# A hybrid attention block on one core: tokens loaded features first, the first norm's factor moved to the products, and four smaller edits

## The chip, the core and the metric

The kernel runs on one core of a Trainium2 chip. The metric is the device time of one execution in microseconds (us). The core has TensorE (PE, with its weight loads PEld), VectorE (DVE), ScalarE (ACT), GpSimd (POOL), and a queue of SyncE (SP) that issues every transfer of this kernel. Each engine works through its own list of instructions in order; an instruction that waits for another engine or for a transfer holds up all that stand behind it on its engine.

## What is computed

One encoder layer on 1024 tokens of 1024 features, cut to its steps:

```python
h = rmsnorm(x, norm_mix)                        # x * rsqrt(mean(x*x) + eps) * gain
proj = h @ w_in                                 # 3384 columns, split into 11 parts
qa, ka, va, qi, ki, wi, qb, kb, vb, gdown, ogate = split(proj)
o_a = dsa_mixer(qa, ka, va, qi, ki, wi)         # index scores, 256 best keys of each query, softmax
o_b = gla_mixer(qb, kb, vb, log_sigmoid(gdown @ w_gate_up + b_gate) / 16)
o_b = rmsnorm(o_b, gla_norm) * silu(ogate)
x = x + concat(o_a, o_b) @ w_out
h = rmsnorm(x, norm_ffn)
x = x + (silu(h @ w_ffn_gate) * (h @ w_ffn_up)) @ w_ffn_down
return rmsnorm(x, norm_final)
```

## The kernel before

Every large product is made of three TensorE passes (`mm3`): each operand is split into a high part, rounded by ACT, and a low part, the rest, made by DVE or POOL. So weights and tokens alike go through "ACT high, then DVE or POOL low" before TensorE can use them.

The order on each engine is fixed ahead by a planner in the kernel (`Flow`): each piece of work is a thread that asks for slots (`pg` pages of SBUF, `ps` four PSUM banks, `pl` two PSUM pairs, `hp` half pages), waits for events, and gives the engine with an assumed duration. The planner emits the instructions in the order of its own clock; on the chip that order stands, and the semaphores make up for what takes longer.

- Beginning. `load_x` brings eight tiles of 128 tokens. `first_norm` takes each tile's sum of squares (ACT and DVE in turn), POOL makes the factor `rstd`, DVE scales the tile (L489). `hidden` transposes it on TensorE (`tp`, L522, 64 transposes of 128x128), and `split_hidden` makes `hT`, high on ACT (L496), low on DVE (L498). `small_weights` gathers 88 narrow columns of `w_in` (`wms`, `wm`). `W` stages weights (`st`), with high on ACT (L257) and low on POOL (L262).
- Products of `main`: `misc` (index keys, index weights and gate, from `wm`) and `index_queries` (`qi`) for each half of the tokens, then `proj_t` (`pj`: value and gate columns) and `proj_f` (`pf`: qb and kb, qa, ka). The `evac_...` functions empty the banks. Behind `misc` and `qi` the index scores start, and `choose` finds the 256th best score of each query by counting, 32 rounds on DVE and ACT at the lowest rank, so it fills DVE.
- `gla` (`pa`, `pk`, `pv`, `po`) runs in between the products; its `att` (L1121) empties the pair that `pk` wants next.
- `softmax` starts with the last product of `ka`: logits `lg` in one of two pairs, emptied by DVE (L1337), then exponent (ACT), reciprocal (DVE), scaling (POOL), transposes `ptr`, and the value products `av`. `combine` adds the two halves of a value sum (`lo`, `so`).
- `out_tiles`, `second_norm` and `scale_tile` (`hr`) make the operands of the feed-forward part, `split_b` splits them (`hc`, low L1629), and `products` and `down` follow.

Of the kernel before, what the change touches and what calls it, by code (L numbers as in the profile page):

```python
# [9 lines left out]
F32 = mybir.dt.float32  # L10
# [315 lines left out]
def block_kernel(ctx: ExitStack, tc: tile.TileContext, a: dict, out: bass.AP, dbg=None):  # L326
# [78 lines left out]
    xs = {}  # L405

    def load_x(i):
        xs[i] = page([P, D], F32, "x")
        nc.sync.dma_start(xs[i], x[i * P:(i + 1) * P, :])

    load_x(0)
    mats = cst.tile([P, 6, P], F32, name="mats")
    nc.sync.dma_start(mats[:, 0:1, :], a["c_mats"][:, 0:1, :])
    ident, tri, flip, cmask = (mats[:, i, :] for i in range(4))
    cmi = mats[:, 4:6, :].rearrange("p a n -> p (a n)").bitcast(I32)
    load_x(1)
    nrm = cst.tile([P, 2, KT], F32, name="nrm")
    wms = page([P, KT, P], F32, "wms")
    nc.gpsimd.memset(wms, 0.0)
    wv = w_in.rearrange("(k p) n -> p k n", p=P)  # L420
    with nc.allow_non_contiguous_dma("small"):
        nc.sync.dma_start(nrm[:, 0, :], a["norm_mix"].rearrange("l (k p) -> p (l k)", p=P))
        load_x(2)
        load_x(3)
        nc.sync.dma_start(wms[:, :, 32:72], wv[:, :, C_KI:C_KI + 40])
        nc.sync.dma_start(wms[:, :, 0:32], wv[:, :, C_KI:C_KI + 32])
        nc.sync.dma_start(wms[:, :, 96:112], wv[:, :, C_GD:C_GD + 16])
    for i in range(4, 8):
        load_x(i)

    def more_loads():

        todo = [(mats[:, 1:, :], a["c_mats"][:, 1:, :]), (wgu[96:112, :], w_gu),
                   (bgt, row_bc(a["b_gate"], 256)), (gnb, row_bc(a["gla_norm"], 512)), (tab, a["rel_bias"]),
                   (nrm[:, 1, :], a["norm_ffn"].rearrange("l (k p) -> p (l k)", p=P))]
        yield At(26000.0)
# [12 lines left out]
    junk_v = cst.tile([P, S], BF16, name="junk_v")  # L449

# [14 lines left out]

    wiT = cst.tile([P, NT * 8], F32, name="wiT")
    fl = Flow()
    ev = fl.event
    pg = Slots(fl, NPG - NT - 1)
    hp, kb, ps, pl = (Slots(fl, n) for n in (NHP, NKB, 4, 2))  # L470
    fl.free[DMA] = 16500.0
# [5 lines left out]
    hT = {}  # L477

# [3 lines left out]
    def first_norm(i):  # L482
        yield At((4500.0, 6050.0, 8650.0, 10000.0, 14000.0, 15250.0, 16700.0, 18200.0)[i])
        yield (ACT, act(S) + 140) if i % 2 == 0 else (DVE, dve(S))
        ss = sumsq(xs[i], i % 2 == 0)
        yield POOL, 730
        r = rstd_of(ss, 1, D)
        yield DVE, 660
        nc.vector.tensor_scalar(xs[i], xs[i], r, None, op0=ALU.mult)  # L489
        ev("xn", i).set()  # L490

    def split_hidden(hf, d, b, give):
# [3 lines left out]
        nc.scalar.activation(t[:, 0, :], b, AF.Copy, scale=nrm[:, 0, d:d + 1])  # L496
        yield DVE, dve(HB) + 60
        nc.vector.scalar_tensor_tensor(t[:, 1, :], b, nrm[:, 0, d:d + 1], f32(t[:, 0, :]),  # L498
                                       op0=ALU.mult, op1=ALU.subtract)
        if give is not None:  # L500
            give.give()
        hT[d, hf] = t
        ev("hT", d, hf).set()

    def hidden(hf):

        step = KT if hf == 0 else 2
        for d0 in range(0, KT, step):
            bs = []
            if hf == 0:  # L510
                for _ in range(4):
                    yield ps
                    bs.append((bank("tp"), ps))
            while len(bs) < step:
                yield pl
                w = wide("tp")
                bs += [(w[:, :HB], None), (w[:, HB:], pl)]
            for j in range(4):
                yield ev("xn", hf * 4 + j)
                for d in range(d0, d0 + step):  # L520
                    yield PE, pe(P, 2)
                    nc.tensor.transpose(bs[d - d0][0][:, j * P:(j + 1) * P], xs[hf * 4 + j][:, d * P:(d + 1) * P],  # L522
# [1834 lines left out]
```

## Time and profile before

| | |
|---|---|
| three runs, median | 1287.97 us (1284.92 to 1291.63) |
| the profiled execution | 1289.89 us, span of its trace 1288.1 us, so 1.8 us lie around it |
| TensorE busy | 1243.2 us, 97% of the span |
| DVE, ACT, POOL busy | 933.7, 600.6, 394.5 us |
| mean granted TensorE clock | 0.985 of full speed |
| moved by DMA | 232.06 MB, 180 GB/s over the span |

The span is what the trace shows from the first to the last instruction. An engine's busy time is summed over its own instructions, so a busy TensorE may still run at the lower clock. The granted clock has two levels here, 1.2 GHz (shown as 0.50) and 2.4 GHz (1.00).

### The profile page before, as it was taken

Reading aid. Unit: us, or ns where it says so; the run is one execution under the profiler, and the core shown is the slowest. Engines: PE = TensorE matmul, PEld = TensorE weight load, DVE = VectorE, ACT = ScalarE, POOL = GpSimd, SP = SyncE. Lnnn points to the kernel's source line nnn. Section 1 sums busy time; section 2 is a strip of 40 time slices with the busy share of each in tenths; the row PEclk is TensorE's granted clock in tenths of the full one; section 3 lists DMA queues with packets and bytes.
Section 4 is the critical chain, followed back from the end, with each engine's and each line's share of the span. In section 5 each row is a group of like instructions: output and inputs, shape, how many; then the busy total and the mean of one; then the engine's idle time right before and its main releaser. Section 6 shows DMA issues by size and latency. Waiting matters only on the chain. (4 is left out here: it accounts for less than half of the span.)

```text
span 1288.1 us, 17923 instructions
## 1 busy us (share of the span) xinstructions
PE 1243.2 (97%) x6074; PEld 1022.6 (79%) x6074; DVE 933.7 (72%) x1739; ACT 600.6 (47%) x1113; POOL 394.5 (31%) x375
## 2 busy tenths in 40 slices
PE   6999999999999999899989999999999999999997
PEld 5878878767787998778868787878888888888885
DVE  6389988979964998843688887768778653335875
ACT  4467777634524787621344444444444332222333
POOL 5324335523401544310103334334333120000340
PEclk8999999979999999999989999999999999999999
DMA  6653221334563437683015777767665479555664
GB/s 212 191 150 123 74 74 42 131 138 152 178 221 100 114 85 201 190 270 129 34 61 184 273 245 258 254 246 261 229 219 205 133 258 379 180 196 190 225 238 164
DMA packets 124909, 232.06 MB, mean 180 GB/s; under 512 B 14297, under 2 KB 72465, under 8 KB 124817
## 3 DMA queue, kind: packets, MB, share of 16 engines
q1 hardware_dynamic: 124816, 230.91, 54.4%
q8 instruction: 48, 0.79, 0.3%
q14 instruction: 45, 0.36, 0.1%
HBM read 148.02 MB, written 82.85 MB: 179 GB/s over the span
## 5 line engine op out<-in xcount | busy, mean ns | idle before, releaser
L1626 POOL TENSOR_TENSOR w<-raw,w 128x512 fp32r<-128x512 f32 x60 | 85.3, 1424 | 214.2 <-ACT w L1766 182.3
L1766 ACT ACTIVATE w<-raw 128x512 fp32r<-128x512 f32 x132 | 81.4, 626 | 54.3 <-DMA d_wd<-wd 15.0
L760 DVE TENSOR_SCALAR_CACHE_REDUCE junk_v<-acc,thr 128x768 bf16<-128x768 f32 (+3 forms) x128 | 103.7, 810 | 2.0
L262 POOL TENSOR_TENSOR w<-st,w 128x512 fp32r<-128x512 f32 x52 | 73.4, 1422 | 75.5 <-ACT w L257 73.3
L767 ACT ACTIVATE junk_a<-acc,thr 128x1024 bf16<-128x1024 f32 x64 | 73.4, 1146 | 46.2 <-DVE thr L784 37.5
L2102 DVE TENSOR_TENSOR da<-U,da 128x512 fp32r<-128x512 f32 x54 | 43.1, 799 | 53.7 <-ACT da L2100 53.5
L2100 ACT ACTIVATE da<-U 128x512 fp32r<-128x512 f32 x54 | 33.7, 630 | 98.8 <-PE da L2156 33.2
L372 PE MATMUL pj<-w,hT 128*128 128x512 f32 x192 | 79.2, 412 | 0.0
L2031 ACT ACTIVATE wd<-wd 128x512 fp32r<-128x512 f32 x77 | 48.3, 629 | 62.1 <-DMA d_wd<-wd 28.1
L373 PE MATMUL pj<-w,hT 128*128 128x512 f32 x192 | 75.9, 395 | 0.0
L374 PE MATMUL pj<-w,hT 128*128 128x512 f32 x192 | 75.8, 395 | 0.0
L372 PE MATMUL pf<-hT,w 128*128 128x512 f32 x192 | 75.8, 395 | 0.0
L1347 POOL TENSOR_SCALAR pb<-pb,sume 128x384 f32<-128x384 f32 (+3 forms) x64 | 47.7, 751 | 89.9 <-DVE sume L1345 74.1
L374 PE MATMUL pf<-hT,w 128*128 128x512 f32 x192 | 74.8, 389 | 0.0
L373 PE MATMUL pf<-hT,w 128*128 128x512 f32 x192 | 74.8, 389 | 0.0
L1807 PE MATMUL fb<-hc,w 128*128 128x512 f32 x176 | 69.5, 395 | 3.9 <-DVE gt L1842 2.5
L1808 PE MATMUL fb<-hc,w 128*128 128x512 f32 x176 | 69.2, 393 | 3.8 <-DVE hc L1629 3.8
L1808 PE MATMUL fc<-hc,w 128*128 128x512 f32 x176 | 69.5, 395 | 2.4 <-DVE hc L1629 2.4
L1807 PE MATMUL fc<-hc,w 128*128 128x512 f32 x176 | 69.1, 392 | 0.4 <-DVE gt L1861 0.4
L2156 PE MATMUL da<-db,da 128*128 128x512 f32 x176 | 68.7, 390 | 0.7 <-DVE da L2102 0.7
L1626 POOL TENSOR_TENSOR wd<-wd 128x512 fp32r<-128x512 f32 x33 | 49.8, 1511 | 63.7 <-ACT wd L2031 55.9
L2154 PE MATMUL da<-db,da 128*128 128x512 f32 x176 | 68.6, 390 | 0.6 <-ACT da L2100 0.6
(315 smaller groups left out, 3643.7 us busy)
## 6 DMA issues: line engine op xcount, KB each, us to landing
d_wd<-wd SPq DMA_DIRECT2D x77, 512.0 KB, 3.5
db<-d_wd SPq DMA_DIRECT2D x77, 512.0 KB, 4.3
st<-w_in SPq DMA_DIRECT2D x52, 256.0 KB, 2.8
raw<-w_ffn_gate SPq DMA_DIRECT2D x22, 512.0 KB, 5.2
raw<-w_ffn_up SPq DMA_DIRECT2D x22, 512.0 KB, 4.5
wd<-w_ffn_down SPq DMA_DIRECT2D x44, 256.0 KB, 4.8
d_ux<-gt SPq DMA_DIRECT2D x9, 512.0 KB, 2.6
d_uy<-gt SPq DMA_DIRECT2D x9, 512.0 KB, 3.5
```

Of the source, the lines that this page charges most:

```text
L262: (eng or self.nc.gpsimd).tensor_tensor(w[:, 1, :], st, f32(w[:, 0, :]), op=ALU.subtract)
L372: mm(ps, lh, rh, start=first, stop=False)
L373: mm(ps, lh, rl, start=False, stop=False)
L374: mm(ps, ll, rh, start=False, stop=last)
L760: v.tensor_scalar(junk_v[:, :w], acc[ts[i]], col, float(S - TOPK), op0=ALU.is_ge, op1=ALU.subtract, accum_out=cnt[:, i:i + 1])
L767: nc.scalar.activation(junk_a[:, :NA[t]], acc[t], AF.Sign, bias=thf[:, nv:], scale=-1.0, accum_out=cnt[:, nv:])
L1626: nc.gpsimd.tensor_tensor(dst, src, high, op=ALU.subtract)
L1766: nc.scalar.activation(w4[:, 0], src, AF.Copy)
L1807: mm(b, w[:, 0, kk], h[:, 0, :], start=first, stop=False, skip_group_check=True)
L1808: mm(b, w[:, 0, kk], h[:, 1, :], start=False, stop=False, skip_group_check=True)
L2154: mm(bs[t], l[:, 0, tt], r[:, 0, :], start=first, stop=False, skip_group_check=True)
L2156: mm(bs[t], l[:, 1, tt], r[:, 0, :], start=False, stop=last, skip_group_check=True)
```

## The change

1. The host lays out a transposed copy of `x` (`c_xt`), the narrow columns (`c_wm`) and the two gains (`c_norms`). `xT` tiles (128 features by 512 tokens) are loaded and split into `hT` without the norm's factor; the scaling by L489 and the 64 transposes are gone. The tokens `x` are loaded too, later, for the sums of squares alone.
2. The factor goes to the products: `rs` as a per-token scale in ACT where tokens lie on partitions; where they lie along the row, `rows` spreads it over 128 partitions (`R`, by eight products of 128x128) and DVE multiplies by it while it empties the bank (`misc`, `qi`, qa, qb, kb, ka). For qa the low part goes from DVE to POOL; for qb and kb the copy goes from ACT to DVE.
3. `W.load()` issues three weight loads ahead of the planner's start, which takes them as there from time 0.
4. `combine` copies half of the value sum, and DVE reads the other half from PSUM; the bank is given back after DVE's sums.
5. The low parts of the last pair of keys (`c == 3`) wait for the first softmaxes.
6. `scale_tile` gives half of its work for tokens 0 to 511 to ACT.
7. Eleven products of 128x512 on a zeroed `junk_a`, whose result nobody reads, stand first on TensorE.

```diff
-    load_x(0)
...
-    nc.gpsimd.memset(wms, 0.0)
...
-        nc.sync.dma_start(wms[:, :, 32:72], wv[:, :, C_KI:C_KI + 40])
...
+    load_xt(0, 0)
+    nc.sync.dma_start(nrm, a["c_norms"])
+    load_wm(0)
+    for k in range(1, 4):
+        load_xt(k, 0)
+    load_wm(1)
+    for k in range(4, KT):
+        load_xt(k, 0)
+    nc.sync.dma_start(mats[:, 0:1, :], a["c_mats"][:, 0:1, :])
+    W.load()
...
+    nc.vector.memset(junk_a, 0.0)
+    idle = wide("idle")
+    for _ in range(11):
+        mm(idle[:, :HB], junk_a[:, :P], junk_a[:, :HB], start=True, stop=True)
...
-    fl.free[DMA] = 16500.0
+    fl.free[DMA] = 12000.0
...
+    def split_hidden(k, hf):
+        if hf == 0:
+            yield At(4500.0 + 650.0 * (k + (k > 3)))
+        else:
+            yield ev("xt", k)
         yield pg
         yield ACT, act(HB) + 42
         t = page([P, 2, HB], F32R, "hT")
-        nc.scalar.activation(t[:, 0, :], b, AF.Copy, scale=nrm[:, 0, d:d + 1])
+        nc.scalar.activation(t[:, 0, :], xT[k, hf], AF.Copy, scale=nrm[:, 0, k:k + 1])
...
+    def load_tokens():
+        W.limit = 4
+        for k in range(KT):
+            if k % 2 == 0:
+                yield pg
+            yield DMA, 650
+            load_xt(k, 1)
+            ev("xt", k).set(2500)
+        for i in range(NT):
+            yield pg
+            yield DMA, 1300
+            xs[i] = page([P, D], F32, "x")
+            nc.sync.dma_start(xs[i], x[i * P:(i + 1) * P, :])
+            ev("x", i).set(2500)
+        W.limit = 8
...
+    def rows():
+        yield pl
+        w = wide("rows")
+        for hf in range(2):
+            yield hp
+            m = half([P, 4, P], F32, "rcol")
             for j in range(4):
...
+                yield ev("rs", i)
+                yield DVE, 250
+                nc.vector.tensor_scalar(m[:, j, :], ident, 0.0, rs[:, i:i + 1], op0=ALU.mult, op1=ALU.add)
+                yield PE, 350
+                mm(w[:, i * P:(i + 1) * P], m[:, j, :], ident, start=True, stop=True)
+            hp.give()
+            yield ACT, act(HB)
+            o = slice(hf * HB, (hf + 1) * HB)
+            nc.scalar.activation(R[:, o], w[:, o], AF.Copy)
+            ev("R", hf).set()
+        pl.give()
...
     def evac_qa(hf, c, b):
...
+        nc.vector.scalar_tensor_tensor(q, b, -0.125, R[:, hf * HB:(hf + 1) * HB], op0=ALU.mult, op1=ALU.mult)
+        ps.give()
         yield ACT, act(HB)
...
+        nc.scalar.activation(t[:, 0, :], q, AF.Copy)
+        yield POOL, pool2(HB)
+        nc.gpsimd.tensor_tensor(t[:, 1, :], q, f32(t[:, 0, :]), op=ALU.subtract)
...
-        yield ACT, act(HB)
-        nc.scalar.activation(dst[i][:, o], b, AF.Copy, scale=0.125 if c < 2 else 1.0)
+        yield DVE, dve(HB)
+        nc.vector.scalar_tensor_tensor(dst[i][:, o], b, 0.125 if c < 2 else 1.0, R[:, o], op0=ALU.mult, op1=ALU.mult)
...
+        nc.vector.tensor_tensor(kf, b, R[:, o], op=ALU.mult)
+        ps.give()
         yield ACT, 2 * act(HB)
...
+        if c == 3:
+            yield ev("p", 2 * PAIRS[0] + 1, 1)
         yield DVE, 2 * dve(HB)
...
-        nc.scalar.activation(lo, OP.pop((p, c)), AF.Copy)
-        ps.give()
+        b = OP.pop((p, c))
+        nc.scalar.activation(lo[64:128, :], b[64:128, :], AF.Copy)
...
+            nc.vector.tensor_tensor(so[e * 64:(e + 1) * 64, :], b[0:64, e * 256:(e + 1) * 256],
                                     lo[64:128, e * 256:(e + 1) * 256], op=ALU.add)
+        ps.give()
...
         for d in range(0, 4, 2):
+            if t and d:
+                yield ACT, 500
+                for i in (d, d + 1):
+                    nc.scalar.activation(hr[(d0 + d) // 2, t][:, i - d, o], b3[:, i, :], AF.Copy,
+                                         scale=nrm[:, 1, d0 + i:d0 + i + 1])
+                continue
             yield DVE, dvf(256)
```

Three places where the order on an engine moves. ACT at the program's beginning, before (`junk_a` is the sum of squares, `wm` the narrow columns, `w<-st` a staged weight's high part):

```order
L460 ACT_TABLE_LOAD
L460 ACTIVATE junk_a,ss<-x 128x1024 x2
L537 ACTIVATE wm<-wms 128x1024
L460 ACTIVATE junk_a,ss<-x 128x1024
L496 ACTIVATE hT<-tp,nrm 128x512 x8
L460 ACTIVATE junk_a,ss<-x 128x1024
L257 ACTIVATE w<-st 128x512 x3
```

and in the changed kernel:

```order
L257 ACT_TABLE_LOAD
L257 ACTIVATE w<-st 128x512 x3
L497 ACTIVATE hT<-xT,nrm 128x512
L574 ACTIVATE wm<-wms 128x512
L497 ACTIVATE hT<-xT,nrm 128x512 x3
L574 ACTIVATE wm<-wms 128x512
L497 ACTIVATE hT<-xT,nrm 128x512 x4
L257 ACTIVATE w<-st 128x512
L497 ACTIVATE hT<-xT,nrm 128x512 x8
L463 ACTIVATE junk_a,ss<-x 128x1024 x2
```

The three staged weights, which stood behind the first eight token splits, now stand ahead of them; on SP their loads are issued behind the ten loads of `xT` and `wms`.

DVE at the first softmaxes, before (the rows of L1257 are the keys' low parts, L1337 empties the logits, L1375 makes low parts for the value products):

```order
L1257 SCALAR_TENSOR_TENSOR K<-pf,K 64x512 x12
L1337 ISA pb,mn<-lg,acc 128x384
L1337 ISA mn 128x1
L1337 ISA pb,mn<-lg,acc 128x512
L1337 ISA mn 128x1
L1345 RECIPROCAL sume<-sume 128x1
L1337 ISA pb,mn<-lg,acc 128x384
L1337 ISA mn 128x1
L1257 SCALAR_TENSOR_TENSOR K<-pf,K 64x512 x4
L1345 RECIPROCAL sume<-sume 128x1 x2
```

and in the changed kernel ahead of the first logit (L1310 multiplies by the factor, L1323 makes the low parts, L883 ends a mask):

```order
L1323 TENSOR_TENSOR K<-kf,K 64x512 x4
L883 TENSOR_SCALAR acc<-sign 128x1024
L1310 TENSOR_TENSOR kf<-pf,rows 128x512 x2
L1323 TENSOR_TENSOR K<-kf,K 64x512 x4
L1310 TENSOR_TENSOR kf<-pf,rows 128x512 x2
L1403 ISA pb,mn<-lg,acc 128x384
```

and behind the fourth:

```order
L1411 RECIPROCAL sume<-sume 128x1
L1403 ISA pb,mn<-lg,acc 128x384
L1403 ISA mn 128x1
L1411 RECIPROCAL sume<-sume 128x1 x2
L1403 ISA pb,mn<-lg,acc 128x512
L1403 ISA mn 128x1
L1411 RECIPROCAL sume<-sume 128x1 x3
L1323 TENSOR_TENSOR K<-kf,K 64x512 x4
L1441 TENSOR_TENSOR pt<-ptr,pt 128x256
L1441 TENSOR_TENSOR pt<-ptr,pt 128x128
L1441 TENSOR_TENSOR pt<-ptr,pt 128x512 x2
```

The four low parts move from behind three logits to behind six, right ahead of the first `pt`; two new multiplications stand ahead of the first logit.

DVE between the last `xn` and the first `hc` of the feed-forward part, before:

```order
L1576 TENSOR_SCALAR xn<-y,rstd 128x1024
L1755 TENSOR_TENSOR raw<-raw,s_6539 128x4x128
L1605 TENSOR_TENSOR hr<-tp,nrm 128x2x128 x2
L1663 TENSOR_TENSOR hr<-hr 128x2x128
L1605 TENSOR_TENSOR hr<-tp,nrm 128x2x128
L1667 TENSOR_TENSOR hr<-hr 128x2x128
L1671 TENSOR_TENSOR hr<-hr 128x2x128
L1629 TENSOR_TENSOR w<-raw,w 128x512
L1629 TENSOR_TENSOR w<-s_5611,w 128x512
L1897 TENSOR_TENSOR gt<-fa,gt 128x512
L1663 TENSOR_TENSOR hr<-hr 128x2x128
L1629 TENSOR_TENSOR w<-s_6539,w 128x512
```

and in the changed kernel:

```order
L1643 TENSOR_SCALAR xn<-y,rstd 128x1024
L1828 TENSOR_TENSOR raw<-raw,s_6573 128x4x128
L1678 TENSOR_TENSOR hr<-tp,nrm 128x2x128
L1702 TENSOR_TENSOR w<-raw,w 128x512
L1702 TENSOR_TENSOR w<-s_5604,w 128x512
L1970 TENSOR_TENSOR gt<-fa,gt 128x512
L1702 TENSOR_TENSOR w<-s_6573,w 128x512
L1702 TENSOR_TENSOR hc<-hr,hc 128x512 x4
```

Two of three `hr` scalings and the sums (L1663 to L1671) have left this stretch; the sums stand ahead of `xn`.

## Rows read from the trace of the kernel before

**Rows 1.** Busy time by stretches of 20 us: each engine, clock, DMA share, GB/s

```profile
core 0: us, PE busy (x) PEld busy (x) DVE busy (x) ACT busy (x) POOL busy (x), PEclk, DMA share, GB/s
0.00:20.00 20.00, 8.63 (x38) 7.39 (x39) 11.05 (x17) 10.21 (x16) 9.86 (x18) 0.92 0.87 271
...
120.00:140.00 20.00, 20.00 (x89) 16.54 (x89) 19.35 (x42) 13.18 (x20) 5.67 (x5) 1.00 0.33 103
...
380.00:400.00 20.00, 20.00 (x89) 16.55 (x89) 5.51 (x8) 4.74 (x8) 0.00 (x0) 1.00 0.42 115
...
640.00:660.00 20.00, 13.76 (x53) 10.16 (x52) 16.65 (x35) 9.96 (x20) 0.00 (x0) 0.88 0.00 1
```

**Rows 2.** Waits of TensorE over the span: releaser, total us, times, longest

```profile
PE tp L522 <- DVE x L489: 9.3, 3, 8.5
PE fb L1808 <- DVE hc L1629: 3.8, 1, 3.8
PE lg L1324 <- DVE mn L1337: 3.1, 2, 2.9
PE pk L1102 <- DVE att L1121: 2.9, 1, 2.9
...
PE fc L1808 <- DVE hc L1629: 2.4, 1, 2.4
...
PE pv L1141 <- DVE bit L774: 1.2, 1, 1.2
```

**Rows 3.** Timeline of the beginning: start, duration, engine, count, idle before and releaser

```profile
4.52 1.06 ACT L460 ACTIVATE junk_a<-x 128x1024 bf16<-128x1024 f32 x1 [2.52 <-DMA x<-x]
...
8.54 3.68 PE L522 MATMUL tp<-mats,x 128*128 128x128 f32 x16 [8.54 <-DVE x L489]
...
17.61 0.79 PE L372 MATMUL misc<-hT,wm 128*128 128x512 f32 x1 [2.55 <-DVE hT L498]
...
34.97 1.06 PE L522 MATMUL tp<-mats,x 128*128 128x128 f32 x8
...
52.42 0.39 PE L372 MATMUL pj<-w,hT 128*128 128x512 f32 x1
```

**Rows 4.** Timeline and tile `st`: splits of tokens and weights, merged runs

```profile
15.48 4.71 ACT L496 ACTIVATE hT<-tp,nrm 128x512 fp32r<-128x512 f32 x8
16.80 5.36 DVE L498 SCALAR_TENSOR_TENSOR hT<-tp,nrm,hT 128x512 fp32r<-128x512 f32 x8
21.08 1.71 ACT L257 ACTIVATE w<-st 128x512 fp32r<-128x512 f32 x3
L262 POOL TENSOR_TENSOR w<-st,w x14: 1285/1292/1847, 22.1 to 51.9; 128x512 fp32r<-128x512 f32 x14
```

**Rows 5.** One microsecond of the token loads

```profile
14.00:15.00 1.00, 1.00 (x9) 0.82 (x8) 1.00 (x1) 0.57 (x1) 0.00 (x0) 1.00 1.03 414
```

**Rows 6.** Three stretches at the lower clock

```profile
17.00:23.70 6.70, 6.09 (x14) 4.79 (x15) 6.70 (x10) 5.79 (x11) 3.58 (x6) 0.50 0.38 130
262.80:276.20 13.40, 13.40 (x58) 8.74 (x57) 7.51 (x25) 3.48 (x7) 1.23 (x2) 0.50 0.10 35
...
648.50:651.70 3.20, 3.20 (x8) 2.52 (x9) 1.74 (x4) 0.00 (x0) 0.00 (x0) 0.50 0.02 5
```

**Rows 7.** Timeline at the first softmaxes

```profile
405.17 2.79 DVE L1257 SCALAR_TENSOR_TENSOR K<-pf,K 64x512 fp32r<-64x512 f32 x4
...
408.25 0.69 DVE L1337 CUSTOM_DVE_ANT_0 pb<-lg,acc 128x512 f32<-128x512 f32 x1
...
414.15 0.72 PE L1384 MATMUL av<-pt,V 128*128 128x256 f32 x4
```

**Rows 8.** DVE's timeline at the beginning of the feed-forward part

```profile
646.75 0.68 DVE L1629 TENSOR_TENSOR hc<-hr,hc 128x512 fp32r<-128x512 f32 x1
...
652.14 0.69 DVE L1849 TENSOR_TENSOR gt<-fc,gt 128x512 f32<-128x512 f32 x1 [1.90 <-PE fc L1809]
...
658.40 0.68 DVE L1629 TENSOR_TENSOR hc<-hr,hc 128x512 fp32r<-128x512 f32 x1
```

**Rows 9.** DVE sums of two operands: `so` from SBUF, `hr` from PSUM (ns; us)

```profile
L1405 DVE TENSOR_TENSOR so<-lo x32: 420/422/1129, 418.6 to 553.2; 64x256 f32<-64x256 f32 x32
638.13 0.42 DVE L1605 TENSOR_TENSOR hr<-tp,nrm 128x256 f32<-128x256 f32 x1
```

More of the change, by code (lines that the diff above doesn't have):

```diff
@@ L449, in block_kernel @@
     junk_v = cst.tile([P, S], BF16, name="junk_v")
+    rs = cst.tile([P, NT], F32, name="rs")
     def rstd_of(ss, n, width):
@@ L502, in split_hidden @@
[L502 to L517, printed above, removed]
-            for j in range(4):
[L519 to L522, printed above, removed]
-                                        ident)
-            for d in range(d0, d0 + step):
-                fl.spawn(split_hidden(hf, d, *bs[d - d0]), 0.01 * d)
-        pg.give(n=4)
@@ L529, in block_kernel @@
-    wm, kw = [], []
-    def small_weights():
-        yield At(11200.0)
-        for _ in range(2):
-            yield pg
-        yield ACT, act(S)
-        wm.extend(page([P, KT, P], F32R, "wm") for _ in range(2))
-        nc.scalar.activation(wm[0], wms, AF.Copy)
-        yield DVE, dve(S)
-        nc.vector.tensor_tensor(wm[1], wms, f32(wm[0]), op=ALU.subtract)
-        pg.give()
-        ev("wm").set()
+        hT[k, hf] = t
+        if k % 2:
+            pg.give()
+        ev("hT", k, hf).set()
@@ new lines, in load_tokens, with first_norm @@
+    def load_tokens():
+        W.limit = 4
+        for k in range(KT):
+            if k % 2 == 0:
+                yield pg
[9 more added lines that the diff above has]
+        W.limit = 8
+    def first_norm(i):
+        yield ev("x", i)
+        yield (ACT, act(S) + 140) if i % 2 == 0 else (DVE, dve(S))
+        ss = sumsq(xs[i], i % 2 == 0)
+        pg.give()
+        yield POOL, 730
+        r = small([P, 1], F32, "rstd", 4)
+        nc.gpsimd.tensor_scalar(r, ss, 1.0 / D, EPS, op0=ALU.mult, op1=ALU.add)
+        nc.gpsimd.tensor_tensor(rs[:, i:i + 1], r, mhalf[:, 0:1], op=ALU.pow)
+        ev("rs", i).set()
@@ L626, in index_queries @@
         bs = []
-        for _ in range(2):
-            yield ps
-            bs.append(bank("qi"))
+        if hf == 0:
+            for _ in range(2):
+                yield ps
+                bs.append(bank("qi"))
+        else:
+            yield pl
+            w = wide("qi")
+            bs = [w[:, :HB], w[:, HB:]]
         for k in range(KT):
@@ L1247, in evac_ka @@
         yield ev("ka page", c)
+        yield hp
+        yield DVE, dve(HB)
+        kf = half([P, HB], F32, "kf")
+        nc.vector.tensor_tensor(kf, b, R[:, o], op=ALU.mult)
+        ps.give()
         yield ACT, 2 * act(HB)
```

154 lines of the change are left out of this document (91 added, 63 removed).

## The prediction

> **What bounds the kernel now.** I read the stretches of 20 us first, then the waits of TensorE, then the timeline at each place where it waits. TensorE is busy in nearly every stretch [rows 1], so only three things are worth time: work taken from TensorE, its waits, and the stretches at the lower clock that follow a wait. Waits worth naming [rows 2]: 9.3 us for the scaled tokens, nearly all before the first product; 2.9 and 1.2 us where the gated block `gla` begins; 2.9 us at the first softmaxes; 2.4 and 3.8 us at the beginning of the feed-forward part. Behind them the clock stands at 1.2 GHz for 6.7, 13.4 and 3.2 us [rows 6], each costing half its length. DVE is the engine that most of these waits are for, and it is full where the scores are chosen, 19.35 of 20 us, and nearly free before the softmaxes, 5.51 of 20 [rows 1].
>
> **The beginning.** Before, the first product starts at 17.61 us and `pj` at 52.42 [rows 3]. What is new is the order on ACT: three staged weights stand ahead of the first token split, and their loads stand on SP behind eight of `xT` and two of `wms`. So ACT waits for thirteen loads of 256 KB and a small one, 3.4 MB. The first load of 512 KB was used at 4.52 us [rows 3]; the other 2.9 MB at 414 GB/s [rows 5] take 7 us, which is 11.5 us; I take 12, since that microsecond is one of the best. Then the last staged weight (1.71/3 = 0.57 us), `hT` and `wm` on ACT (4.71/8 = 0.59 each) and two low parts on DVE (5.36/8 = 0.67 each) [rows 4]: 12 + 0.57 + 1.18 + 0.7 (the first low part hides behind `wm`'s high part) is about 14.6 us. Start: 3.0 us earlier, not the ten that loads in feature order would allow.
>
> From there to `pj` TensorE has the same products. The 64 transposes are gone; 32 of them ran before 17.61 us and don't count, the other 32 stood between products at 1.06/8 = 0.13 us [rows 3], 4.3 us, with about 0.4 us of wait for scaled tokens (9.3 - 8.5 = 0.8 us for the two shorter waits [rows 2], of which I count one). Added are eight products for `rows`, at 0.13 to 0.23 us each by the same transposes at either clock (3.68/16 [rows 3]), 1.4 us in the middle. Gain to `pj`: 3.0 + 4.7 - 1.4 = **6.3 us**, if nothing else is late there. Next in line is the factor `R`: it holds three banks that `pj` wants. The second halves of `xT` go behind three more weight loads, which wait on SP for POOL's low parts (1.29 us each [rows 4]); I put their end at 24.6 us, and the eight tiles of `x` behind them, 4.2 MB, at 35. Sum of squares (1.06 us [rows 3]) and the rest end some 3 us later, 38, and the `rows` products stand in `qi`, which runs from some 34 to 46 us. The margin is a few us. Bounds of the term: 4 us (loads at 300 GB/s, a wait for `R`) to 9 (TensorE at full clock from its first product).
>
> The eleven idle products need only DVE's memset, so at half clock, 0.45 us each, they end by about 6 us; TensorE then has nothing until 14.6 us. Before, a gap of 2.55 us ahead of the first product [rows 3] was followed by 6.7 us at the lower clock [rows 6]. I count the idle products at nothing, and the slow stretch as before.
>
> **Evacuations.** qb and kb move eight copies from ACT to DVE, and `ka` and the small ones add multiplications, each like the 0.69 us of one DVE pass over 128x512 [rows 7]; 8 x 0.69 = 5.5 us of this falls where DVE is full [rows 1]. Counting has the lowest rank, so it slides: the last mask comes later by that and by the `ka` work ahead of it, into the stretch with 14 us free [rows 1]. A bank is given back after one DVE pass, and the two banks of a group are wanted again only after 48 products of 20/89 = 0.225 us [rows 1], 11 us. So nothing on the path. POOL gets eight low parts of qa, 8 x 1.29 = 10.3 us, ahead of `gla`'s decays, which starts `gla` later among the products; all its products still stand ahead of `ka`'s end. Cost 0, but see the rivals.
>
> **Where `gla` begins.** `pk` waits for the pair that `att` empties, behind DVE's counting: 2.9 us, then 1.2, and 13.4 us at half clock [rows 2, 6], 10.8 us in all. In the new order `pk` stands one group of three products (0.68 us) behind `pa`, before it was two. DVE is as full as it was. I take the same stall and 0.7 us more: **+0.7**, bounds -10.8 (DVE comes in time) to +11 (a second such stall).
>
> **First softmaxes.** The four low parts of 2.79 us stood in front of the fourth logit, and TensorE waited 2.9 us [rows 2, 7]. Now they stand behind six logits, but two multiplications (1.4 us) stand ahead of the first. In a replay by hand with the durations of the trace, the transposes start some 1.3 us earlier; then the low parts, now right in front of the first `pt`, hold up `av` by 2.4 us, and `av` begins where it did, at 414.15 [rows 7]. The stall moves: **0**, bounds -3 to +2.
>
> **Value sums.** The same number of instructions on ACT and DVE; the bank is held for two sums more, about 0.9 us. What a sum costs with one operand in PSUM is bounded by its neighbours: 0.42 us for 256 columns from SBUF, and 0.42 us for 256 columns from PSUM [rows 9]. So 0, bounds -1 to +2. [...]
>
> **Feed-forward.** Between the last `xn` and the first `hc`, DVE loses five sums and two scalings of 0.34 to 0.42 us, but still waits for `fa`. The low part of `hc`, which ended TensorE's first wait at 646.75 [rows 8], comes about 0.7 us earlier. The next DVE work then waited 1.90 us for `fc` [rows 8], which ran at the lower clock for 3.2 us [rows 6]. With a shorter gap I take that fall as avoided (1.6 us), and two scalings fewer follow (0.3 us on this chain). The `hc` of 658.40 [rows 8] then comes 0.7 + 1.6 + 0.3 = 2.6 us earlier: **-2.5**, bounds 0 to -6 (the second wait shrinks as well).
>
> **Sum.** -6.3 + 0.7 + 0 + 0 - 2.5 = -8.1 us on the profiled execution's 1289.9, which gives 1281.8. That execution is 1.9 us above the median of the three runs, so I predict 1287.97 - 8.1, about **1280 us**.
>
> **The rivals.**
> - *DVE in time at `gla`.* The stall and its slow stretch vanish: the counting stands elsewhere by a few instructions, and the wait was of 3 us only. Against it: DVE is no emptier. 1280 - 11 = 1269. Chance 0.15.
> - *The factor late.* `x` comes behind everything, in-order SP holds loads behind POOL's low parts, and `R` holds three of four banks; from the point where `R` is ready later than 46 us, `pj` waits. At 300 GB/s the 4.2 MB take 14 us instead of 10, and the front's gain falls to some 1 to 2 us: 1285. Chance 0.14.
> - *DVE as the one that frees banks (slower).* Every bank of `pf` now hangs on a DVE pass in a queue that is 97% full. It decides once DVE lags TensorE by more than the 11 us of a group, or `gla` runs into the evacuation of `ka`, whose pages it holds: its last product now stands right ahead of `ka`'s first, with 11 us to spare. Each such place costs a stall like the one at `gla`, 10.8 us; two of them give 1280 + 21.6 = 1302. For it speaks the full DVE and the added 10 us on POOL; against it that DVE's counting slides. Chance 0.13.
> - *The change does what it says.* ACT doesn't hold the token splits, the first product starts at about 6 us behind the idle products at full clock, and the front gains up to 16 us, cut by `R` to some 12: 1274. Against it stands the order on ACT. Chance 0.05.
>
> **How the numbers follow.** My forecast has chance 0.53, with its own range 1274 to 1287. A measurement of this kernel tells about 0.5% from no change, so faster means below 1281.5 and slower above 1294.4. Of the forecast 0.33 lies below 1281.5 and 0.20 above; with 0.15 and 0.05 from the early rivals, faster has 0.53; with the late factor the same has 0.34; slower 0.13. For 8 in 10 the range takes in the rival at `gla` and one extra stall of 10.8 us: 1268 to 1292.
>
> **What the changed profile would show.** Right: the first token split on ACT at about 12.6 us behind a wait for `st`; the first `misc` product near 14.6; `pj` near 46; a wait at the first `pk` followed by half clock; no gain at the first `av`; the first `hc` wait without a slow stretch behind it. Wrong: a first product by 8 us, a `pj` that waits for a bank, `pf` products that wait for DVE's multiplications, or a `gla` stall that is gone or double; the last two alone move the total by more than all else here.

## The result and the profile after

The changed kernel takes **1298.41 us** (median of 6 runs, 1297.56 to 1302.18) against 1286.45 for the kernel before on the same chip: ratio **1.0104**, 95% interval 1.0078 to 1.0130. That is slower by about 1%, above the whole predicted range, where a gain had been forecast. The profiled execution took 1302.18 us with a span of 1300.4; before it was 1289.9 and 1288.1.

The span falls into stages, each from the first product of one kind to that of the next (`pj`, `pf`, `lg`, `fa`, `da`). They are read from TensorE's timeline, in us:

| kernel | beginning | scores, to `pf` | `pf` and `gla` | attention | feed-forward |
|---|---|---|---|---|---|
| before | 52.4 | 110.7 | 238.7 | 231.0 | 436.5 |
| changed | 50.5 | 116.4 | 239.7 | 242.3 | 432.9 |
| difference | -1.9 | +5.7 | +1.0 | +11.3 | -3.6 |
| predicted | -6.3 | 0 | +0.7 | 0 | -2.5 |

Two stages that I had put at nothing, the attention and the scores, made most of the result; the beginning, which gained 4.4 us less than forecast, made the rest. TensorE's waits over the whole span, the counterpart of [rows 2] (releaser, us in total, times, longest):

```profile
PE misc L372 <- ACT wm L574: 10.4, 1, 10.4
PE pk L1161 <- DVE att L1180: 5.3, 1, 5.3
PE fb L1881 <- DVE hc L1702: 3.8, 1, 3.8
PE ptr L1426 <- DVE so L1471: 3.3, 3, 1.2
PE av L1450 <- DVE ptl L1441: 3.2, 2, 2.6
PE av L1450 <- issue: 2.6, 1, 2.6
PE oa L373 <- DVE w L262: 2.3, 3, 1.2
PE dots L751 <- ACT relu L754: 2.0, 2, 1.6
PE dots L751 <- DMA qst<-d_qi: 1.9, 1, 1.9
```

The first wait has about the size of the one it replaces (9.3 in [rows 2]). New are the wait of the attention (`ptr`) for the value sums `so` and the waits of the scores (`dots`); the wait of `av` for low parts (`ptl`) was 1.6 us before. The wait at `lg` is gone, and one of 2.6 us at the first `av` has come for it ("issue": the profile shows no releaser).

The beginning, from the timeline (start, duration, engine, count, idle before), and then the windows of 4 us (TensorE, weight loads, DVE, ACT, POOL, granted clock, DMA share, GB/s), beside [rows 3, 6]:

```profile
1.48 4.88 PE L472 MATMUL idle<-junk_a 128*128 128x512 bf16 x11 [1.48 <-DVE junk_a L469]
...
13.53 2.01 ACT L257 ACTIVATE w<-st 128x512 fp32r<-128x512 f32 x3 [11.53 <-DMA st<-w_in]
15.44 0.71 ACT L497 ACTIVATE hT<-xT,nrm 128x512 fp32r<-128x512 f32 x1
...
16.72 0.80 PE L372 MATMUL misc<-hT,wm 128*128 128x512 f32 x1 [10.37 <-ACT wm L574]
...
17.20 1.76 DVE L576 TENSOR_TENSOR wm<-wms,wm 128x512 fp32r<-128x512 f32 x1
...
50.49 0.47 PE L372 MATMUL pj<-w,hT 128*128 128x512 f32 x1
```

```profile
4.00:8.00 4.00, 2.35 (x6) 0.61 (x4) 0.00 (x0) 0.00 (x0) 0.00 (x0) 1.00 0.91 274
8.00:12.00 4.00, 0.00 (x0) 0.00 (x0) 0.00 (x0) 0.00 (x0) 0.00 (x0) 0.71 1.07 387
12.00:16.00 4.00, 0.00 (x0) 0.00 (x0) 0.00 (x0) 2.35 (x4) 2.06 (x3) 0.50 0.26 82
16.00:20.00 4.00, 2.40 (x4) 1.36 (x5) 3.82 (x4) 4.00 (x8) 2.41 (x2) 0.50 0.63 148
20.00:24.00 4.00, 4.00 (x12) 3.13 (x11) 4.00 (x6) 2.68 (x5) 1.28 (x1) 0.58 0.94 286
```

ACT did nothing for 11.53 us and then ran the three staged weights; the token splits stood behind them. The idle products had been over at 6.4 us, and the granted clock had fallen to half (0.50) before the first real product.

### The profile page after: what moved, and what is told of

It is laid out like the page before. It is cut to its first block, busy times and chain, and to the rows that moved or that the text cites. A ratio compares the mean times of both kernels' runs of the same rounds, so it can differ in the third digit from the quotient of the medians.

```text
span 1300.4 us, 17906 instructions
## 1 busy us (share of the span) xinstructions
PE 1242.8 (96%) x6037; PEld 1014.8 (78%) x6037; DVE 950.8 (73%) x1755; ACT 610.3 (47%) x1122; POOL 405.6 (31%) x382
## 5 line engine op out<-in xcount | busy, mean ns | idle before, releaser
L1699 POOL TENSOR_TENSOR w<-raw,w 128x512 fp32r<-128x512 f32 x60 | 88.1, 1470 | 208.5 <-ACT w L1839 174.7
L814 DVE TENSOR_SCALAR_CACHE_REDUCE junk_v<-acc,thr 128x512 bf16<-128x512 f32 (+3 forms) x128 | 103.4, 808 | 2.2
L821 ACT ACTIVATE junk_a<-acc,thr 128x1024 bf16<-128x1024 f32 x64 | 73.3, 1146 | 58.9 <-DVE thr L838 51.1
L262 POOL TENSOR_TENSOR w<-st,w 128x512 fp32r<-128x512 f32 x52 | 70.3, 1361 | 84.2 <-ACT w L257 71.7
L1881 PE MATMUL fb<-hc,w 128*128 128x512 f32 x176 | 69.8, 397 | 3.8 <-DVE hc L1702 3.8
L1880 PE MATMUL fb<-hc,w 128*128 128x512 f32 x176 | 69.9, 397 | 1.7 <-DVE gt L1915 1.7
L1882 PE MATMUL fb<-hc,w 128*128 128x512 f32 x176 | 69.4, 395 | 0.0
```

The costliest lines, as they stand in the source:

```text
L262: (eng or self.nc.gpsimd).tensor_tensor(w[:, 1, :], st, f32(w[:, 0, :]), op=ALU.subtract)
L814: v.tensor_scalar(junk_v[:, :w], acc[ts[i]], col, float(S - TOPK), op0=ALU.is_ge, op1=ALU.subtract, accum_out=cnt[:, i:i + 1])
L821: nc.scalar.activation(junk_a[:, :NA[t]], acc[t], AF.Sign, bias=thf[:, nv:], scale=-1.0, accum_out=cnt[:, nv:])
L1699: nc.gpsimd.tensor_tensor(dst, src, high, op=ALU.subtract)
L1880: mm(b, w[:, 0, kk], h[:, 0, :], start=first, stop=False, skip_group_check=True)
L1881: mm(b, w[:, 0, kk], h[:, 1, :], start=False, stop=False, skip_group_check=True)
```

## The experiments

Each run was timed beside the kernel before on the same chip; ratios are to that. The stages of the other profiles stand in one table at the end of this section.

**The value sums: the hold, or the order?** The first run keeps the changed kernel's order on every engine and takes away only the longer hold of the bank:

```diff
-        nc.scalar.activation(lo[64:128, :], b[64:128, :], AF.Copy)
+        nc.scalar.activation(lo, b, AF.Copy)
...
-            nc.vector.tensor_tensor(so[...], b[0:64, ...], lo[64:128, ...], op=ALU.add)
+            nc.vector.tensor_tensor(so[...], lo[0:64, ...], lo[64:128, ...], op=ALU.add)
```

> The changed kernel, in its own order on every engine, but the value sums again read a whole copy of the bank in SBUF, so the bank is free after ACT's copy and no longer after DVE's two sums. Theory A (the longer hold of the bank is what the attention lost): the waits of ptr and av for the sums (about 4.5 us in the changed kernel) go, and with them what they delay; 1298.4 falls by 4 to 10 us, to 1288 to 1294. Theory B (the order that the planner wrote around the new costs is the loss, not the hold): 1297 to 1299, and the waits that go come back at other places. Theory C (a sum with one operand in PSUM is itself dearer): the DVE sums measure shorter than 0.42 us here, and the time falls by 1 to 2 us.

Measured: 1298.55 us, ratio 1.0119 (1.0097 to 1.0140). Nothing was gained in time, though the attention of its profile is 2.5 us shorter than the changed kernel's (239.8 for 242.3). Its sums, read from SBUF, took DVE 492 ns on average instead of 418, 2.4 us in all, so a cost of the hold of about that size could hide behind them. The second run also plans the sums as before (`ps.give()` behind the copy), so that the order of the attention changes; up to the first `av` the order stays that of the changed kernel.

> The changed kernel with the value sums as before, planned as before too, so the order around them differs from the changed kernel's. Theory A: the same as the run with the changed kernel's order, within 3 us (1288 to 1294). Theory B: the attention gets back its 12 us and the time is 1286 to 1289, clearly below the run that keeps the order. Theory D (the attention lost by what comes ahead of it, such as the K lows or the later bank): no gain, 1296 to 1300.

Measured: 1291.52 us, ratio 1.0059 (1.0041 to 1.0076), some 6 to 7 us less, and the attention took 232.7 us. TensorE's waits in the attention, first with the changed kernel's order and no hold, then planned anew:

```profile
PE ptr L1426 <- DVE pt L1441: 4.0, 2, 2.1
PE av L1450 <- issue: 2.6, 1, 2.6
```

```profile
PE av L1450 <- issue: 2.6, 1, 2.6
PE oa L373 <- DVE w L262: 1.5, 3, 0.7
PE av L1450 <- DVE ptl L1441: 1.5, 2, 1.2
PE ptr L1426 <- DVE pt L1441: 1.1, 2, 0.7
```

With the hold taken away the wait for `so` (3.3 us) is gone, but `ptr` waits 4.0 us for the next thing that DVE brings. The order is what costs: the two runs hold the same instructions, and only the plan differs. Where it differs is seen in the output products `oa`, the only work there that doesn't hang on the softmaxes still running. Their windows of 6 us at the end of the attention (TensorE busy with `oa`, count, clock, DMA share, GB/s), the changed kernel first, then the one planned anew:

```profile
542.00:548.00 6.00, 3.06 (x14) 1.00 0.31 96
548.00:554.00 6.00, 1.06 (x5) 1.00 0.95 275
554.00:560.00 6.00, 0.00 (x0) 0.94 0.47 154
560.00:566.00 6.00, 4.23 (x9) 0.50 0.33 98
```

```profile
538.00:544.00 6.00, 3.58 (x15) 1.00 0.42 130
544.00:550.00 6.00, 0.00 (x0) 1.00 0.73 223
550.00:556.00 6.00, 3.35 (x9) 0.80 0.74 238
```

In both, 60 of these products run before the last `av`. In the changed kernel 48 of them are used up when 24 `av` are left, and then none comes from 549 to 562 us; in the other order 36 are used up there, and twelve more stand behind the next four `av` (541 to 543 us). So the last heads have less to hide behind, and an `av` waits longer for its low part:

```profile
558.19 0.38 PE L1450 MATMUL av<-ptl,V 128*128 128x256 f32 x1 [2.63 <-DVE ptl L1441]
```

```profile
546.71 0.39 PE L1450 MATMUL av<-ptl,V 128*128 128x256 f32 x1 [1.22 <-DVE ptl L1441]
```

The low part itself was late for a transfer. In the changed kernel DVE stood still ahead of it until a store of finished value sums (`d_ma<-mxa`), issued at 550.0 us, had landed at 557.6:

```profile
557.71 0.62 DVE L1441 TENSOR_TENSOR ptl<-ptr,pth 128x256 fp32r<-128x256 f32 x2 [2.94 <-DMA d_ma<-mxa]
```

In the order planned anew no store holds DVE there. From the first `oa` to the last `av` the changed kernel takes 43.0 us, the one planned anew 37.2. Of these 5.8 us, 3.5 are more idleness and 1.7 are the clock, which stands at 0.50 for 6.8 us there instead of 3.4. The other 4 us lie ahead of the first `oa`.

Is it the sums' edit alone? The same edit in the kernel before:

> The kernel before with one edit alone: the value sums read one half from the PSUM bank, which is given back after DVE's two sums, and the order is planned for that. Theory B (the order planned around the longer hold costs the attention some 6 to 10 us): 6 to 10 us slower than the kernel before, all of it between the first logit and the last output product. Rival (the edit is harmless where the rest of the order is as before, and only its meeting with the deferred K lows costs): within 2 us of the kernel before.

Measured: 1292.78 us, ratio 1.0048 (1.0025 to 1.0071), some 6 us slower, the attention at 237.9 instead of 231.0. And is it the late bank in the planner's book, or would any other order cost as much? Three runs change only the planned cost of a sum, by 27 ns, which gives another order each time: in the run planned anew, in the changed kernel (there the other way round) and in the kernel before:

```diff
-            yield DVE, dve(256)
+            yield DVE, dvf(256) - 60
```

> The changed kernel with the sums from a whole copy and the bank planned as free after the copy, but with the changed kernel's planned cost of a sum (27 ns more). Another order in the attention (132 of TensorE's instructions elsewhere), the same work. Theory (the bank that the planner believes late is what makes the order bad): 1289 to 1294, as the run with the old cost (1291.5). Rival (the planner's order scatters by several us with any number): anywhere from 1286 to 1300, and no nearer to the old cost than to the changed kernel.

> The changed kernel, bank held and planned late as in it, with the former planned cost of a sum (27 ns less). Another order in the attention (173 of TensorE's instructions elsewhere), the same work. Theory (late bank): 1296 to 1300, as the changed kernel. Rival (scatter): as far from the changed kernel as the early-bank run was, below 1294 or above 1302.

> The kernel before with the changed kernel's planned cost of a value sum (27 ns more) and nothing else: another order in the attention from its second half on (98 of TensorE's instructions elsewhere), the same work and the bank still free after the copy. Theory (early bank): the attention stays at 231 to 235 us and the time within 3 us of the kernel before. Rival (any other order than this one costs, whatever the bank): 5 us slower or more, the attention at 237 or above, as with the sums' edit alone (237.9).

Measured: bank planned early, 1293.62 us, ratio 1.0071 (1.0047 to 1.0095), attention 233.8; planned late, 1300.00 us, ratio 1.0120 (1.0097 to 1.0143), attention 242.2; the kernel before with the other cost, 1285.56 us, ratio 1.0019 (1.0003 to 1.0035), attention 232.0. Over all twenty profiles, the ten with the bank planned as free after the copy have an attention of 231.0 to 235.9 us (mean 232.6), the ten with the bank planned late 237.9 to 243.2 (mean 241.0). The groups don't touch: **8.5 us for the late bank in the plan**, with single profiles up to 3.3 us from their group's mean. The place of the loss is the same in all of them: from the first `oa` to the last `av` the first ten take 35.6 to 38.7 us, the others 40.4 to 43.0, and when 24 `av` are left, 36 of the 60 output products are used up in each of the first ten and 48 in each of the others. In nine of the late ten (not in the run with the hold away) DVE stands 2.2 to 3.4 us for such a store there, in the early ten never over 1.0. No run moves the twelve products or the store alone, so what each of them is worth is read from the order, not tested apart.

**What held the beginning.**

```diff
     nc.sync.dma_start(mats[:, 0:1, :], a["c_mats"][:, 0:1, :])
-    W.load()
```

> The changed kernel without the three weight loads that were put in the program ahead of the token splits; they are issued by the planner behind them. Theory A (ACT was held by the staged weights): the first product starts at 6 to 8 us instead of 16.7; the factor still comes at 44 us, and pj waits for banks, so the first pj moves from 50.5 only to 45 to 48 and the time falls by 2 to 5 us, to 1293 to 1296. Rival (the factor is no limit): the first pj comes at 40 us and the time falls by 9 to 11. Rival (the token splits were held by their own loads): the first product stays near 14 us and nothing changes.

Measured: 1288.70 us, ratio 1.0038 (1.0018 to 1.0058), 8 to 10 us less than the changed kernel, where 2 to 5 were expected. The first product starts at 6.28 us. The first `pj` moves by only 4 us, to 46.5. On the way there TensorE waits 1.6 us at the `rows` products, which need the factor, but 3.8 us at `qi` for the parts of its weights (2.6 for POOL's low parts, 1.2 for ACT's high parts), so the factor alone isn't the limit that I expected. The rest of the gain comes from the stages behind (the table): 2.7 us in the scores and 7.0 in `pf` and `gla`, where the wait at `pk` shrinks from 5.3 to 1.6 us and the 6.8 us at half clock behind it are gone. Is it ACT's order or also SP's? The next run leaves the loads where they are and tells the planner that they land 12 us later:

```diff
-            staged.put(st)
+            staged.put(st, 12000.0)
```

> The changed kernel with its three staged loads where they are in SP's order, but the planner is told that they land 12 us later than it believed, so it puts their three passes on ACT behind the first token splits. Theory (ACT's order held up the beginning): the first product at 6 to 7 us as without the staged loads, and 6 to 9 us faster than the changed kernel. Rival (the loads on SP, ahead of the second halves, hold it up as well): the first product at 6 to 7 us, but the first pj at 49 to 51 and a gain of under 3 us.

Measured: 1292.35 us, ratio 1.0055 (1.0038 to 1.0071): first product at 6.34, `pj` at 47.0, scores 114.1, each within half a microsecond of the run without staged loads. ACT's order alone held up the beginning; this run differs from the other by 6 us in `gla` (a `pk` wait of 3.8 us in all, and 13.7 us at half clock behind it where the other has none), not there.

**The factor, the lows, the idle products, the scaling.** One edit each in the changed kernel: the factor's row set to 1 from the start, with the products that make it left out (so this run leaves the factor out of what it computes); the wait `if c == 3` ahead of the K lows taken out; no idle products; no scaling on ACT.

> The changed kernel with the row of the norm's factor set to 1 at the beginning and the eight products that make it left out, so nothing waits for the factor that the feature-major products take (the per-token factor of the other products is still computed). Theory A (the late factor holds up the index keys and queries, and so the scores, which stretch from 123 to 138 us): the waits for relu, nb and qst go, the first pf comes at 161 to 163 us instead of 166.9, and the time falls by 4 to 6 us. Theory B (the scores lost by their order and by DVE, not by the factor): the first pj comes 1 us earlier and the first pf stays above 165; the time falls by 1 us.

Measured: 1299.80 us, ratio 1.0128 (1.0106 to 1.0150), the scores at 118.3, with 3.4 us of them at half clock. The late factor isn't what the scores lost. But the run doesn't clear it wholly either: TensorE waits 4.5 us for `qst` loads in it, 2.6 more than in the changed kernel.

> The changed kernel with the K lows of the last keys made at once, as before, instead of behind the first two softmaxes. Theory (the stall only moved): the wait of 2.6 us at the first av goes, one of 2 to 3 us at a logit comes back, and the time stays within 1.5 us of the changed kernel. Rival (the put-off lows upset DVE's order in the attention): 3 to 8 us faster than the changed kernel.

Measured: 1295.66 us, ratio 1.0083 (1.0059 to 1.0106); the wait at `av` is replaced by 3.0 us at `lg`, and some 2 to 3 us are gained, with intervals that overlap. In the version with both repairs the same edit gains nothing (below).

> The changed kernel without the eleven idle products. There TensorE stands 10.4 us between them and the first real product, and the slow stretch ends at the same 23.8 us as in the kernel before. Theory: they are worth nothing, the time stays within 1.5 us of the changed kernel, and the clock rises at 23 to 24 us here too. Rival: the rise and fall of the clock at the beginning lengthens the slow stretch, and the time falls by 2 to 3 us without them.

Measured: 1299.83 us, ratio 1.0118 (1.0094 to 1.0141). No difference.

> The changed kernel with the scalings of the last tiles all on DVE, as before. The feed-forward part took 432.9 us in the changed kernel and 436.5 in the one before; in the kernel before, the edit alone gave only 1 us of this. If ACT's share of the scalings is the cause here: the part takes 435 to 437 us again and the time is 2 to 4 us above the changed kernel. If it is another cause (the order that the planner writes for this part after another beginning): 432 to 434 us and the time within 1.5 us.

Measured: 1299.66 us, ratio 1.0115 (1.0093 to 1.0136), and the feed-forward part still takes 432.6 us. The scaling isn't what that stage gained. The same edit alone in the kernel before:

> The kernel before with one edit alone: half of the scalings of the last four tiles on ACT instead of DVE. Theory (this edit is what the feed-forward part gained): that part, from its first product fa to the first da, takes 432 to 434 us instead of 436.5, and the time falls by 3 to 4 us. Rival (the gain came from another phase in which the attention ended): no change within 1 us, and the part stays at 436.

Measured: 1285.22 us, ratio 0.9990 (0.9967 to 1.0014), the stage at 435.5. No difference.

**A version that beats both.** No staged weights, and the sums from a whole copy:

> The changed kernel with both repairs: no staged weights ahead of the token splits, and the value sums from a whole copy, planned so. If the two losses are separate, their gains add: 8.5 us (front and what follows it) and 6 us (attention), so about 14 us faster than the changed kernel, which is within 2 us of the kernel before or up to 3 faster. Rival (the gains share a cause, such as the phase in which the attention begins): no more than 9 us faster than the changed kernel.

Measured: **1278.38 us, ratio 0.9943** (0.9916 to 0.9970), and in a second set of runs:

> The version with both repairs once more: the changed kernel without staged weights ahead of the token splits, and with value sums from a whole copy, planned so. If the first measurement holds: 0.992 to 0.997 of the kernel before, about 1278 us. If it was a lucky set: 0.998 to 1.002, as the version with another planned cost.

Measured: **1279.49 us, ratio 0.9964** (0.9949 to 0.9979). The two repairs add up or do a little better, 18 to 21 us below the changed kernel by these ratios where the two alone make some 14, and what is left of the change is 5 to 7 us faster than the kernel before. Three relatives of this version: lows at once, no idle products, another planned cost of the sums.

> The version with both repairs (no staged weights ahead of the token splits, value sums from a whole copy), and the K lows of the last keys made at once, as before. In the changed kernel this alone gave 2.7 us back. If that was the lows' own doing: 2 to 4 us faster than the version with both repairs, 1275 to 1276, with the wait of 2.6 us at the first av gone and a shorter one at a logit. If it was the meeting with the sums' order: within 1.5 us of 1278.

> The version with both repairs, without the eleven idle products at the beginning. There the first real product follows them at 6.3 us and runs at 2.4 GHz from the first. Theory (the idle products are worth something only where real products follow at once): without them the first stretch of real products runs at 1.2 GHz for 3 to 7 us; its products take longer, but what follows waits for loads and for the factor, so the first pj moves by less than 1.5 us and the time by less than 2. Rival (every slow microsecond counts): 3 us slower.

> The version with both repairs (no staged weights, sums from a whole copy), with a planned cost of a sum 87 ns higher: another order in the attention (283 of TensorE's instructions elsewhere), the same work. Theory (early bank, the order scatters little): 1276 to 1281, as the version with both repairs (1278.4). Rival (scatter): 1274 or less, or above 1283.

Measured: 1280.92 us, ratio 0.9974 (0.9956 to 0.9992); 1280.59 us, ratio 0.9967 (0.9954 to 0.9980); and 1284.85 us, ratio 0.9998 (0.9978 to 1.0018). The first two can't be told from the version itself. The third is slower by some 4 to 7 us: its attention takes 235.9 us and waits for other things (2.1 us for `pt`, 1.5 for `lo`). That is some 4 us more than in the version itself. Its profile, which is 3.5 us above the median of its runs, also has 236.6 us in `pf` and `gla`, some 4.6 more, in a stretch whose order is the same; so an equal-looking order of the planner gives back part of the gain, and how much of the loss is the order is not shown.

The stages of these profiles, in us (L: bank planned late):

| kernel | beginning | scores | `pf`, `gla` | attention | feed-forward |
|---|---|---|---|---|---|
| changed, hold away, same order (L) | 51.1 | 115.7 | 236.9 | 239.8 | 433.5 |
| sums planned as before | 53.7 | 116.1 | 236.9 | 232.7 | 432.7 |
| sums planned as before, other cost | 50.8 | 116.2 | 238.6 | 233.8 | 432.4 |
| changed, other cost (L) | 52.0 | 116.4 | 239.7 | 242.2 | 432.0 |
| no staged weights (L) | 46.5 | 113.7 | 232.7 | 243.2 | 431.5 |
| planner told late (L) | 47.0 | 114.1 | 238.8 | 241.6 | 431.6 |
| factor known (L) | 48.8 | 118.3 | 236.0 | 243.2 | 435.6 |
| lows at once (L) | 50.2 | 117.7 | 239.1 | 239.8 | 432.2 |
| no idle products (L) | 49.5 | 117.2 | 238.6 | 240.1 | 432.5 |
| scaling as before (L) | 49.4 | 119.4 | 238.3 | 240.3 | 432.6 |
| before + sums (L) | 52.1 | 112.1 | 234.6 | 237.9 | 435.9 |
| before + scaling | 52.6 | 112.4 | 236.0 | 232.4 | 435.5 |
| before, other cost | 52.5 | 112.0 | 233.2 | 232.0 | 436.3 |
| both repairs | 46.4 | 112.6 | 231.9 | 232.3 | 432.4 |
| both, again | 45.9 | 115.7 | 232.1 | 231.7 | 432.6 |
| both, lows at once | 46.8 | 114.2 | 231.9 | 232.0 | 436.1 |
| both, no idle products | 46.6 | 113.6 | 232.1 | 231.8 | 436.3 |
| both, other cost | 46.8 | 116.6 | 236.6 | 235.9 | 431.9 |

## Why the prediction was wrong

**Value sums: the step that failed.** I took "the bank is held for two sums more, about 0.9 us" and concluded "So 0". The instructions were as I said: DVE's sum takes no longer with one operand in PSUM (the changed kernel's sums; shortest, median, longest in ns), beside 420/422/1129 in [rows 9].

```profile
L1471 DVE TENSOR_TENSOR so<-av,lo x32: 416/417/421, 422.7 to 569.4; 64x256 f32<-64x256 f32 x32
```

No run shows the 2 us of that term's upper bound as a price of the operand in PSUM: the median sum takes 417 ns against 422. And the hold itself, in an unchanged order, cost nothing that the time shows (ratio 1.0119 without it, 1.0104 with it). What I left out is that the program's order is written by a planner that reads the same hold: between the plan with the late bank and the one with the early bank, 558 of the 6037 places in TensorE's list hold another product by the names in the traces, and the new order took twelve output products from the last heads and put one of their low parts behind a store that took 7.6 us to land. An edit of the planner's book has to be read in the order it writes, not in the duration of its instructions. The attention lost 11.3 us in the two profiles, and the late bank in the plan makes 8.5 of it by the groups. Beside it two terms were mis-sized: the scores, put at nothing, lost 5.7 us, and the beginning fell 4.4 us short.

**The beginning: the mechanism right, the size off.** ACT was held by the staged weights, as forecast; without them the first product starts at 6.3 us. The first term missed by 2.1 us (16.7 for 14.6): at 13.5 us the first of the three staged loads was there, and ACT could begin with the last of them only at 14.9, rather than 12. The low part in the sum (0.7 us) stood in nobody's way, since the first product waited for the high part of `wm` alone. The second term missed by 2.3: from the first product to `pj` TensorE took 33.8 us instead of the 31.5 that the sum implies. The 32 transposes between products were worth 3.1 us (from each one's start to the next product's, waits in between included), not 4.7; the `misc` products took 0.7 us longer, with a wait of 0.9 us for the low part of `wm`; `qi` took 0.2 us longer, and `rows` 1.2 us instead of 1.4. The rival in which the change does what it says named 6 us for the first product, and without the staged weights that came true; its gain of 12 us at `pj` didn't: 5.9 us against the kernel before, 46.5 for 52.4.

**Evacuations: wrong by a stage.** I put them at 0, "nothing on the path". The scores lost 5.7 us. TensorE's waits there, which the kernel before hadn't:

```profile
PE dots L751 <- ACT relu L754: 2.0, 2, 1.6
PE dots L751 <- DMA qst<-d_qi: 1.9, 1, 1.9
PE dots L751 <- DVE nb L1004: 0.7, 1, 0.7
```

They make 4.6 of it; the last score product starts at 138.1 us instead of 122.8. In all runs the stage takes 110.7 to 112.4 us with the old front, 112.6 to 116.6 with the new one and ACT free, and 115.7 to 119.4 with ACT held. Eight of the profiles with the new front spend 1.5 to 6.8 us of the stage at half clock. With half of that taken off, the ranges are 110.7 to 112.4, 112.3 to 114.1 and 115.3 to 116.6 (means 111.8, 113.1 and 116.0), and the last two no longer touch. So the held splits explain some 3 us of it. A late factor was not shown to be the rest, and the eight copies moved to DVE weren't tried apart. That rest, 1.3 us between the means, stays open.

**`gla`: right in size by luck.** +0.7 forecast, +1.0 measured, but I took the same stall, and it wasn't: TensorE's idleness in the stage grew from 3.9 to 7.3 us (the wait at `pk` from 2.9 to 5.3), while the slow stretch behind it was half as long, 6.8 us instead of 13.7. The two cancel. The slower rival, DVE as the one that frees banks, was the right side by another mechanism: no second stall came here, and its 1302 us are a coincidence.

**First softmaxes: right.** The stall moved, and DVE makes the four low parts (413.6 to 416.8 us) right ahead of it, as forecast: it went from `lg` (2.9) to the first `av` (2.6, where I had 2.4), and from the first `lg` to the first `av` it takes 11.0 us instead of 12.3.

**Feed-forward: near in size, for the most part by luck.** -2.5 forecast, -3.6 measured. Up to TensorE's second wait the forecast holds: the first wait, at `fc`, fell from 2.4 to 1.9 us, no slow stretch follows it, and the product behind the second wait, which stays at 3.8 us, starts 24.2 us behind the first `fa` instead of 26.3, 2.1 us earlier where 2.6 were forecast. But the slow stretch behind the second wait is then 6.8 us long instead of 3.4, which takes 1.7 us back. In the kernel before with the scaling alone it is the same (24.2 and 6.8), which is why that run gains next to nothing. The rest of the -3.6 is that TensorE idles 2.1 us behind the second wait instead of 4.4. That isn't the scaling's doing: the stage is 435.6 to 436.3 us in three runs with the new front and 431.5 to 433.5 in the others, with 3.0 to 4.3 and 1.2 to 2.1 us of this idleness. What sets it stays open.

**The idle products** were worth nothing, as forecast: ratio 1.0118 without them, 1.0104 with them. The staged loads made sure of it.

## What to carry to other kernels

Where a planner writes the order, an edit that changes what the planner believes (a bank free later, a load there sooner) must be judged by the order that comes out: here a bank that the plan gives back later cost 8.5 us of the attention, 5.5 of them in its last heads (42.2 for 36.7 on average), with DVE's sums no slower (417 ns for 422). A model that believes staged data ready at time zero puts its consumers ahead of all that is ready in truth: here ACT, which works in the order given, stood still for 11.5 us. A small change of a planned cost gives a control: how much a version scatters by order alone, before a few microseconds are put down to an edit.

## What the runs showed of the hardware

At a granted clock of 0.50, products of 128x512 follow each other 0.427 us apart (265.35 to 266.63 us of the kernel before), at 1.00 some 0.227 us (120.06 to 120.51 us). So 512 columns in 427 ns make 1.2 columns a ns at 0.50; the names 1.2 and 2.4 GHz for the two levels are an estimate from that, at one column a period and twice as much.

The slow stretch behind a stall had no fixed length for a given stall in these runs. The same order and the same wait at `pk` (2.94, 2.95, 2.93 and 2.97 us) stood in four kernels with the old front. Two of them also have the same second wait, at `pv` (1.16 and 1.20 us): the kernel before and the one with the scaling alone. Windows of 8 us of these two, in this order (clock third from the end):

```profile
256.00:264.00 8.00, 6.84 (x45) 4.53 (x43) 7.86 (x20) 2.75 (x5) 1.47 (x1) 0.92 0.90 319
264.00:272.00 8.00, 8.00 (x38) 5.05 (x33) 4.98 (x16) 1.84 (x3) 1.23 (x2) 0.50 0.03 11
272.00:280.00 8.00, 8.00 (x40) 5.81 (x40) 3.56 (x10) 2.71 (x5) 1.97 (x2) 0.73 0.01 2
```

```profile
256.00:264.00 8.00, 6.80 (x43) 4.61 (x41) 7.96 (x17) 2.38 (x5) 3.35 (x3) 1.00 0.68 236
264.00:272.00 8.00, 8.00 (x39) 5.22 (x38) 4.84 (x16) 3.08 (x5) 1.23 (x2) 0.57 0.25 96
272.00:280.00 8.00, 8.00 (x53) 5.91 (x53) 6.53 (x21) 2.60 (x5) 1.98 (x2) 1.00 0.10 38
```

The first stands at half clock for some 13.7 us, the second for some 6.8, though TensorE is busy all the while in both; the stage takes 238.7 and 236.0 us. The other two, without the second wait, stand there for 6.8 and 3.4 us (234.6 and 233.2). By the first two, a stage time of one profile with a stall in it is known to some 3 us, no better.

Sums with both operands in SBUF took up to 1.25 us now and then (60 of 352 over all profiles took more than 0.45), those with one operand in PSUM never over 0.42. In the traces the long ones stand beside POOL: each of the 60 started while a POOL instruction was at work, nearly always the scaling of `pb`, and ended 0.27 to 0.28 us behind the end of that instruction. Of the 288 sums with an operand in PSUM, 82 started beside POOL in the same way, and none of them took longer.
